# A hybrid retention and sliding-window layer on one core: the position bias table in and out of 128 partitions, and the projections' products and rotation sums moved from GpSimd to VectorE

## The chip, the core and the metric

The kernel runs on one core of a Trainium2 chip. The core has a TensorE (PE; its weight loads are listed apart, as PEld), a VectorE (DVE), a ScalarE (ACT), a GpSimd (POOL) and a SyncE (SP), which here issues most of the DMAs; 16 DMA engines move the data. The metric is the device time of one execution in microseconds; the time of a kernel is the median of its runs.

## What is computed

One step of a layer of width 1024 over 1024 prompt and 64 sample positions (1088 columns together), all in float32. What matters here is the first third of it: one combined projection of the normalized input, retention, and sliding-window attention with a relative position bias.

```python
def retention_qkv(rq, rk, rv, pos):
    q = rope(rq.reshape(B, S, RET_HEADS, RET_DK), pos)
    k = rope(rk.reshape(B, S, RET_HEADS, RET_DK), pos) * (RET_DK ** -0.5)
    v = rv.reshape(B, S, RET_HEADS, RET_DV)

def rope(x, pos):
    x1, x2 = xf[..., :half], xf[..., half:]
    return jnp.concatenate([x1 * cos - x2 * sin, x2 * cos + x1 * sin], axis=-1)

def in_proj(x, g_attn, w_in):
    return jnp.split(rms_norm(x, g_attn) @ w_in, SPLIT_OFFS, axis=-1)

def rel_bias_block(table, n_q, n_past):
    rel = (j - n_past) - i
    ...
    b = table[bucket]
    return jnp.transpose(b, (2, 0, 1)).reshape(SWA_KV_HEADS, SWA_GROUP, n_q, n_past + n_q)
```

Retention has 4 heads of 256; the window attention has 16 query heads of 64 on 2 key heads, a bias by distance from a table of 32 x 16 numbers, and a sink per head. Behind them follow gates, an output mix, cross attention to 256 memory rows, a SwiGLU of width 2816 and a last normalization.

## The kernel before

**The data.** Activations lie transposed: features on the 128 partitions, the 1088 columns along the free axis, in two halves of 544 columns. A float32 operand is split into a rounded part (ScalarE, L124) and the rest (VectorE, L125), and a product is three matmuls, one after the other (L223, L224, L226 for the large ones, L157 to L159 for the rest).

**The large projections** go in pairs of 128-row weight tiles through a Strassen scheme (`strassen`): seven products of 512 x 544 instead of eight. Sums of weight quarters (L191 to L197 on VectorE; L201 to L207 on GpSimd once `sums_by` is set to it) and their splits (wq) are made just ahead. A product fills a pair of PSUM banks called pq, of which there are three; it leaves them through a copy (ScalarE, L277) or a sum on VectorE (L274, L613), the latter into one of eight staging tiles called stage, each 128 x 544. A staging tile can be used anew when the store of what it held has landed.

**project_phase** makes, in the order of the code: v of head 0; then for each head h of 0 to 3 its k and q (`rotated`), for h > 0 its v, and one pair of the window attention's query rows (`project` with w_sq, stored to d_sq); the retention of that head (`retention`), block by block of 256 columns; at h = 1 the bias table, queued for a later moment; then the window attention's keys and values, the last query pair, and the gates. The retention of a head runs beside the projections of the next: its matmuls are mixed into PE's order among the large products, and its other steps into the orders of VectorE and ScalarE.

**Rotation** (`rotated`). With both rows a and b of a head's half in staging tiles, VectorE makes the four products with sine and cosine (L644 to L647). The difference (L649) and the sum (L650) are on VectorE for heads 0 and 1 and on GpSimd for heads 2 and 3. SP then stores both to d_qkv in DRAM, from where `retention` loads them as ks and qs, and the values as vf.

**The factor 1/rms** (rstd, spread over partitions by L512 and copied by ScalarE, L514) is multiplied to the window attention's queries, keys and values on GpSimd (L619, 20 instructions), and to the gates, which have an activation, on VectorE (the same line).

**Retention** of a block transposes ks and vf on PE (L768) into small PSUM banks (two of them, called r), from where ScalarE and VectorE scale and split them (L799, L800, L808, L809); then come the scores (pss), the state (pkv) and the output (po). `ret_out` normalizes the output through a chain of short VectorE steps (L893, L320 to L329) and ScalarE (L896), and PE transposes it back (L902).

**The bias table** (`bias_table`, L564 to L577): a one-hot matrix of 32 x 256 and the 32 x 16 table make 16 rows of 256 numbers, one per query head; they are scaled, written twice side by side (rb, 16 partitions of 2 KB) and stored 32 times over to d_rb, 16 rows of 64 KB. The window attention reads d_rb much later, with a row step that turns the repetition into the shift by distance.

**The order.** Tile, the layer that records the kernel, decides by its own model of times in which order instructions stand on each engine; each engine then goes through its order strictly, and so does SP with its DMAs. Hence moving an instruction from one engine to another can reorder the instructions around it on all engines.

Of the kernel before, what the change touches and what calls it, by code (L numbers as in the profile page):

```python
# [11 lines left out]
F32 = mybir.dt.float32  # L12
F32R = mybir.dt.float32r
AF = mybir.ActivationFunctionType
ALU = mybir.AluOpType
# [4 lines left out]
P = 128  # L20
# [7 lines left out]
BLK = 256  # L28
# [81 lines left out]
class Kernel:  # L110
# [453 lines left out]
    def bias_table(self):  # L564

        nc, io = self.nc, self.io
        t = self.ra.tile([P, BLK + 16], F32, tag="sf", bufs=1, name="table")
        rb = self.ra.tile([P, 2, BLK], F32, tag="o", bufs=1, name="rb")[:16]
        table, onehot = t[:32, BLK:], t[:32, :BLK]
        self.load(table, io["rel_bias"])  # L570
        self.load(onehot, io["c_onehot"])
        pb = self.norm_psum("pb")
        nc.tensor.matmul(pb[:16, :256], table, onehot, start=True, stop=True)
        nc.vector.tensor_scalar(rb, pb[:16, :256].unsqueeze(1).broadcast_to([16, 2, 256]), 8.0, None, ALU.mult)
        self.store(self.d_rb.rearrange("h (i c) -> h i c", c=512),
                   rb.rearrange("p a b -> p (a b)").unsqueeze(1).broadcast_to([16, 32, 512]))
        row = self.np.tile([P, 16], F32, tag="row", bufs=1, name="row")[:1]  # L577
        self.load(row, io["sinks"])
        ps = self.norm_psum("ps")
        nc.tensor.matmul(ps[:, :16], self.ones[:1, :], row, start=True, stop=True)  # L580
        for e in range(2):
            rows = slice(e * 64, (e + 1) * 64)
            nc.vector.tensor_copy(self.sinks[rows, :], ps[rows, :16].rearrange("p (a b) -> p a b", b=2)[:, :, e])
        self.minus = self.np.tile([P, 16], F32, tag="row", bufs=1, name="minus")[:, :NPAIR]
        nc.vector.tensor_scalar(self.minus, self.sinks, -1.0, None, ALU.mult)

    def project_phase(self):
        nc, tc, io = self.nc, self.tc, self.io
        with ExitStack() as ctx:
# [11 lines left out]
            half = lambda t: slice(t * HALF, (t + 1) * HALF)  # L601
# [14 lines left out]
            def project(w, put, act=None, other=None):  # L616
                def emit(i, t, ps, sb):
                    o = taken(ps, sb)
                    (nc.vector if act is not None else nc.gpsimd).tensor_tensor(  # L619
                        out=o, in0=o, in1=self.rstd[:, half(t)], op=ALU.mult)  # L620
                    if act is not None:
                        nc.scalar.activation(o, o, act)
                    if other is not None:
                        r = op.tile([P, HALF], F32, tag="other", bufs=4, name="other")
                        self.load(r, other(i)[:, half(t)])
                        nc.gpsimd.tensor_tensor(out=o, in0=o, in1=r, op=ALU.mult)
                    put(i, t, o)
                cast = self.last_cast
                self.strassen(w, self.ops, emit)
                return cast  # L630

            def rotated(w, h, j, before=None):
# [3 lines left out]
                def emit(i, t, ps, sb):  # L636
# [3 lines left out]
                    a, b = done[0, t], done[1, t]  # L640
                    cos, sin = (rope[:, i, half(t)] for i in range(2))
                    sa, sb = flat(staged()), flat(staged())
                    tt = nc.vector.tensor_tensor
# [1 line left out]
                    tt(out=sb, in0=b, in1=sin, op=ALU.mult)  # L645
                    tt(out=a, in0=a, in1=cos, op=ALU.mult)
                    tt(out=b, in0=b, in1=cos, op=ALU.mult)  # L647
                    tt = tt if h < 2 else nc.gpsimd.tensor_tensor
                    tt(out=a, in0=a, in1=sb, op=ALU.subtract)  # L649
                    tt(out=b, in0=b, in1=sa, op=ALU.add)  # L650
                    self.store(self.d_qkv[j, 2 * h, :, half(t)], a)
# [69 lines left out]
            for idx, w, act in ((1, "w_ga", AF.Sigmoid), (0, "w_rg", AF.Silu), (2, "w_gb", AF.Sigmoid)):  # L721
                for m in range(0, KT, 2):
                    if (idx, m) == (1, 6):
# [4 lines left out]
                        op = ctx.enter_context(tc.tile_pool(name="op", bufs=1, reuse_waits="tile"))  # L728
# [1164 lines left out]
```

## Time and profile before

| | us |
|---|---|
| median of 3 runs | 2172.07 (2171.89 to 2172.37) |
| the profiled execution | 2170.14 |
| its span | 2168.3 |
| PE busy | 2134.6 (98%) |
| DVE busy | 1547.7 (71%) |
| ACT busy | 875.0 (40%) |
| POOL busy | 588.8 (27%) |

The profile is of one execution; times in its views are microseconds from the start of its span. A row of a timeline has start, duration, engine, line, operation, tiles (out<-in) and, in brackets, how long the engine had been idle before and what ended that. A row of a group has the number of instructions, their busy time and mean duration in ns, and behind the second bar the idle time ahead of them with what ended it. Engines overlap instructions that follow each other, so that their starts can lie closer than a duration.

### The profile page before, as it was taken

Reading aid. Unit: us, or ns where it says so; the run is one execution under the profiler, and the core shown is the slowest. Engines: PE = TensorE matmul, PEld = TensorE weight load, DVE = VectorE, ACT = ScalarE, POOL = GpSimd, SP = SyncE. Lnnn points to the kernel's source line nnn. Section 1 sums busy time; section 2 is a strip of 40 time slices with the busy share of each in tenths; the row PEclk is TensorE's granted clock in tenths of the full one; section 3 lists DMA queues with packets and bytes.
Section 4 is the critical chain, followed back from the end, with each engine's and each line's share of the span. In section 5 each row is a group of like instructions: output and inputs, shape, how many; then the busy total and the mean of one; then the engine's idle time right before and its main releaser. Section 6 shows DMA issues by size and latency. Waiting matters only on the chain. (4 is left out here: it accounts for less than half of the span.)

```text
span 2168.3 us, 41740 instructions
## 1 busy us (share of the span) xinstructions
PE 2134.6 (98%) x16371; PEld 2082.8 (96%) x16371; DVE 1547.7 (71%) x2874; ACT 875.0 (40%) x1896; POOL 588.8 (27%) x484
## 2 busy tenths in 40 slices
PE   9999999999999999999999999999999999999997
PEld 9999999999999997889999999999999999999997
DVE  8986978776677558656545565778777777877597
ACT  8333434353434357543233333333322222344243
POOL 0001211233253124540000000015556555523531
PEclk9999999999999999999999999999999999999998
DMA  7334453444345476336442121522342333384333
GB/s 268 118 128 120 135 140 104 138 126 154 120 142 178 154 228 218 119 108 209 133 147 96 40 69 46 161 67 91 126 149 89 105 117 100 117 311 151 112 116 112
DMA packets 169894, 290.84 MB, mean 134 GB/s; under 512 B 39298, under 2 KB 96546, under 8 KB 169698
## 3 DMA queue, kind: packets, MB, share of 16 engines
q1 hardware_dynamic: 161666, 269.00, 38.8%
q0 software_dynamic: 3424, 10.82, 1.4%
q10 hardware_dynamic: 4608, 8.36, 1.0%
q8 instruction: 129, 2.11, 0.4%
q14 instruction: 67, 0.55, 0.1%
HBM read 196.95 MB, written 91.16 MB: 133 GB/s over the span
## 5 line engine op out<-in xcount | busy, mean ns | idle before, releaser
L125 DVE TENSOR_TENSOR wq<-raw,wq 128x512 fp32r<-128x512 f32 (+1 forms) x499 | 435.4, 877 | 131.8 <-ACT wq L124 128.2
L124 ACT CAST wq<-raw 128x512 fp32r<-128x512 f32 (+1 forms) x499 | 301.8, 614 | 539.8 <-PE pq L226 210.5
L224 PE MATMUL pq<-T,wq 128*128 128x272 f32 x1832 | 492.2, 289 | 0.1
L223 PE MATMUL pq<-T,wq 128*128 128x272 f32 x1832 | 490.7, 288 | 1.3 <-DVE stage L613 0.6
L224 PE MATMUL pq<-B,wq 128*128 128x272 f32 x1592 | 427.0, 288 | 0.1
L223 PE MATMUL pq<-B,wq 128*128 128x272 f32 x1592 | 425.7, 288 | 0.0
L226 PE MATMUL pq<-T,wq 128*128 128x272 f32 x1832 | 382.9, 289 | 1.9 <-DVE wq L125 1.9
L223 PEld LDWEIGHTS pq<-T,wq 128*128 128x128 f32 x1832 | 344.4, 188 | 2.1 <-ACT xsq L499 0.8
L224 PEld LDWEIGHTS pq<-T,wq 128*128 128x128 f32 x1832 | 344.2, 188 | 1.2 <-issue 0.8
L226 PE MATMUL pq<-B,wq 128*128 128x272 f32 x1592 | 331.7, 289 | 0.0
L224 PEld LDWEIGHTS pq<-B,wq 128*128 128x128 f32 x1592 | 299.1, 188 | 0.8 <-issue 0.4
L223 PEld LDWEIGHTS pq<-B,wq 128*128 128x128 f32 x1592 | 299.0, 188 | 0.1
L226 PEld LDWEIGHTS pq<-T,wq 128*128 128x128 f32 x1832 | 289.8, 189 | 3.9 <-DVE wq L125 2.4
L201 POOL TENSOR_TENSOR raw<-raw 128x512 f32<-128x512 f32 (+1 forms) x44 | 62.2, 1413 | 802.4 <-DVE rs_r L322 455.6
L226 PEld LDWEIGHTS pq<-B,wq 128*128 128x128 f32 x1592 | 251.7, 189 | 0.9 <-issue 0.7
L274 DVE TENSOR_TENSOR u<-pq,u 128x544 f32<-128x544 f32 x177 | 127.2, 719 | 84.8 <-PE pq L226 84.6
L619 POOL TENSOR_TENSOR stage<-stage,rstd 128x544 f32<-128x544 f32 x20 | 31.6, 1584 | 323.0 <-ACT rstd L514 203.7
L613 DVE TENSOR_TENSOR stage<-pq,u 128x544 f32<-128x544 f32 x112 | 80.3, 718 | 31.6 <-PE pq L226 27.8
L157 PE MATMUL pd<-xc,wq 128*128 128x256 f32 (+1 forms) x256 | 74.5, 291 | 0.0
L1541 POOL TENSOR_TENSOR stage<-stage,rstd_f 128x544 f32<-128x544 f32 x40 | 63.9, 1607 | 39.1 <-ACT stage L1540 39.1
L159 PE MATMUL pd<-xc,wq 128*128 128x256 f32 (+1 forms) x256 | 74.1, 290 | 0.0
L158 PE MATMUL pd<-xc,wq 128*128 128x256 f32 (+1 forms) x256 | 73.7, 288 | 0.0
(391 smaller groups left out, 4587.2 us busy)
## 6 DMA issues: line engine op xcount, KB each, us to landing
hl<-d_op SPq DMA_DIRECT2D x85, 272.0 KB, 5.1
d_qkv<-stage SPq DMA_DIRECT2D x44, 272.0 KB, 2.2
d_op<-stage SPq DMA_DIRECT2D x44, 272.0 KB, 2.5
d_op<-ht SPq DMA_DIRECT2D x44, 272.0 KB, 3.6
raw<-w_gate SPq DMA_DIRECT2D x22, 512.0 KB, 3.5
raw<-w_up SPq DMA_DIRECT2D x22, 512.0 KB, 5.1
raw<-w_down SPq DMA_DIRECT2D x16, 512.0 KB, 4.9
d_gate<-stage ACTq DMA_DIRECT2D x28, 272.0 KB, 2.8
```

The lines of the kernel that those rows point to most:

```text
L124: self.last_cast = self.nc.scalar.copy(hi, src).ins
L125: return self.nc.vector.tensor_tensor(out=lo, in0=src, in1=hi.bitcast(F32), op=ALU.subtract).ins
L157: mm(ps, wh, xh, start=start, stop=False)
L158: mm(ps, wh, xl, start=False, stop=False)
L159: self.last_mm = mm(ps, wl, xh, start=False, stop=stop).ins
L201: tt(out=a11, in0=a11, in1=a21, op=sub)
L223: mm(ps[:, c, :HC], w[:, 0, ks], x[:, 0, cs], start=start, stop=False)
L224: mm(ps[:, c, :HC], w[:, 0, ks], x[:, 1, cs], start=False, stop=False)
L226: self.last_mm = mm(ps[:, c, :HC], w[:, 1, ks], x[:, 0, c * HC:(c + 1) * HC], start=False, stop=stop).ins
L274: add = lambda out, a, b: nc.vector.tensor_tensor(out=out, in0=a, in1=b, op=ALU.add)
L613: nc.vector.tensor_tensor(out=o, in0=ps, in1=sb, op=ALU.add)
L1541: nc.gpsimd.tensor_tensor(out=g, in0=g, in1=r[t], op=ALU.mult)
```

## The change

It has three edits.

1. The table of the bias gets each of its columns 8 times in the input array (32 x 128 instead of 32 x 16), the matmul makes 128 rows instead of 16, and the scaled rows lie in 128 partitions. The store writes each partition 4 times over instead of 32, to the same 16 x 64 KB in the same order.
2. The products with rstd in `project` are on VectorE in all cases.
3. The rotation's difference and sum are on VectorE for all heads.

```diff
-        t = self.ra.tile([P, BLK + 16], F32, tag="sf", bufs=1, name="table")
-        rb = self.ra.tile([P, 2, BLK], F32, tag="o", bufs=1, name="rb")[:16]
+        t = self.ra.tile([P, BLK + P], F32, tag="sf", bufs=1, name="table")
+        rb = self.ra.tile([P, 2, BLK], F32, tag="o", bufs=1, name="rb")
         table, onehot = t[:32, BLK:], t[:32, :BLK]
...
-        nc.tensor.matmul(pb[:16, :256], table, onehot, start=True, stop=True)
-        nc.vector.tensor_scalar(rb, pb[:16, :256].unsqueeze(1).broadcast_to([16, 2, 256]), 8.0, None, ALU.mult)
-        self.store(self.d_rb.rearrange("h (i c) -> h i c", c=512),
-                   rb.rearrange("p a b -> p (a b)").unsqueeze(1).broadcast_to([16, 32, 512]))
+        nc.tensor.matmul(pb[:, :256], table, onehot, start=True, stop=True)
+        nc.vector.tensor_scalar(rb, pb[:, :256].unsqueeze(1).broadcast_to([P, 2, 256]), 8.0, None, ALU.mult)
+        self.store(self.d_rb.rearrange("h (r i c) -> (h r) i c", r=8, i=4),
+                   rb.rearrange("p a b -> p (a b)").unsqueeze(1).broadcast_to([P, 4, 512]))
...
-                    (nc.vector if act is not None else nc.gpsimd).tensor_tensor(
-                        out=o, in0=o, in1=self.rstd[:, half(t)], op=ALU.mult)
+                    nc.vector.tensor_tensor(out=o, in0=o, in1=self.rstd[:, half(t)], op=ALU.mult)
...
-                    tt = tt if h < 2 else nc.gpsimd.tensor_tensor
                     tt(out=a, in0=a, in1=sb, op=ALU.subtract)
                     tt(out=b, in0=b, in1=sa, op=ALU.add)
...
-    arr["rel_bias"] = a["rel_bias"]
+    arr["rel_bias"] = np.repeat(a["rel_bias"], 8, axis=1)
```

The lines behind the second edit stand one higher, those behind the third two higher: L644 to L647 become L643 to L646, the sums L649 and L650 become L647 and L648, and L768 becomes L766.

The orders of all engines differ between the place of the first moved product (at 204 us of the profile before) and the last one (at 499 us); ahead of it and behind it they are the same. Three places show how.

VectorE where the first query pair is projected (beside head 2's k). Before, its four products stand on GpSimd, and VectorE has:

```order
L125 TENSOR_TENSOR wq<-raw,wq 128x512
L193 TENSOR_TENSOR raw<-raw 128x512
L274 TENSOR_TENSOR u_3002<-pq,u_3000 128x544
L125 TENSOR_TENSOR wq<-raw,wq 128x512
L904 COPY ret_t<-pb 128x2x64
```

With the change:

```order
L125 TENSOR_TENSOR wq<-raw,wq 128x512
L193 TENSOR_TENSOR raw<-raw 128x512
L619 TENSOR_TENSOR stage_640<-stage_640,rstd 128x544 x4
L274 TENSOR_TENSOR u_3002<-pq,u_3000 128x544
L125 TENSOR_TENSOR wq<-raw,wq 128x512
L902 COPY ret_t<-pb 128x2x64
```

The four products now stand between a weight sum and the sum L274 that empties a bank.

VectorE a little later, at the rotation of head 2's first row pair, beside the retention of head 1. Before:

```order
L646 TENSOR_TENSOR stage_639<-stage_639,rope 128x544
L125 TENSOR_TENSOR wq<-raw,wq 128x512
L125 TENSOR_TENSOR qs<-qs 128x512
L125 TENSOR_TENSOR ss<-sf,ss 128x384
L645 TENSOR_TENSOR stage_640<-stage_640,rope 128x544
L125 TENSOR_TENSOR st<-state,st 128x512
L125 TENSOR_TENSOR wq<-raw,wq 128x512
L647 TENSOR_TENSOR stage_640<-stage_640,rope 128x544
L125 TENSOR_TENSOR ks<-ks 128x512
```

With the change (L645, L644 and L646 are the products above, L647 and L648 the sums):

```order
L645 TENSOR_TENSOR stage_639<-stage_639,rope 128x544
L648 TENSOR_TENSOR stage_639<-stage_639 128x544
L125 TENSOR_TENSOR qs<-qs 128x512
L644 TENSOR_TENSOR stage_640<-stage_640,rope 128x544
L125 TENSOR_TENSOR ss<-sf,ss 128x384
L647 TENSOR_TENSOR stage_639<-stage_639,stage_640 128x544
L125 TENSOR_TENSOR wq<-raw,wq 128x512
L646 TENSOR_TENSOR stage_640<-stage_640,rope 128x544
L647 TENSOR_TENSOR stage_639<-stage_639,stage_640 128x544
L125 TENSOR_TENSOR st<-state,st 128x512
L125 TENSOR_TENSOR ks<-ks 128x512
```

The sums stand among the splits of the retention of head 1 and of the weights. PE's order follows: the matmuls of head 1's retention stand further back among the large products (its last one behind 1920 matmuls of L223 to L226 instead of 1779), those of head 2 likewise, and from the retention of head 3 on they stand nearly where they stood.

SP around the store of the table (d_rb), with the query pair's stores (d_sq) and the loads of head 2's second block (vf, ks, qs). Before:

```order
L121 DMA d_ret<-ret_t 128x2x64
L121 DMA d_rb<-rb 512x1x512
L121 DMA d_sq<-stage_640 128x32
L121 DMA d_sq<-stage_640 128x8x64
L121 DMA d_sq<-stage_640 128x32
L121 DMA d_sq<-stage_640 128x8x64
L118 DMA vf<-d_qkv 128x2x256
L121 DMA d_sq<-stage_640 128x8x64
L121 DMA d_sq<-stage_640 128x32
L118 DMA raw<-w_q 128x1024
L118 DMA ks<-d_qkv 128x2x256
L118 DMA qs<-d_qkv 128x2x256
```

With the change:

```order
L121 DMA d_sq<-stage_640 128x8x64 x2
L121 DMA d_sq<-stage_640 128x32
L118 DMA raw<-w_q 128x1024
L121 DMA d_ret<-ret_t 128x2x256
L118 DMA table<-rel_bias 32x128
L118 DMA table<-c_onehot 32x256
L118 DMA raw<-w_q 128x1024
L121 DMA o_rss<-state 128x2x256
L121 DMA d_ret<-ret_t 128x2x64
L121 DMA d_rb<-rb 512x1x512
L118 DMA vf<-d_qkv 128x2x256
L118 DMA ks<-d_qkv 128x2x256
```

The query pair's stores and the loads of the next weight now stand ahead of the table's store, and the loads of head 2's second block directly behind it.

## The prediction

> **What bounds the kernel now.** I read the page first, then the busy times by stretch, then PE's waits in the stretch that the change touches. In the rows by stretch the columns are busy microseconds and instruction counts of PE, PEld, DVE, ACT and POOL, then granted clock, DMA share and GB/s.
>
> ```profile
> PE 2134.6 (98%) x16371; PEld 2082.8 (96%) x16371; DVE 1547.7 (71%) x2874; ACT 875.0 (40%) x1896; POOL 588.8 (27%) x484
> ```
>
> PE is busy for 98% of the span. The change removes no product from PE, so it can win only time in which PE stands still.
>
> ```profile
> 100.00:200.00 100.00, 100.00 (x800) 97.75 (x800) 80.04 (x167) 42.01 (x95) 0.00 (x0) 1.00 0.39 122
> 196.00:266.00 70.00, 67.41 (x536) 65.62 (x536) 61.77 (x109) 28.03 (x63) 19.18 (x12) 1.00 0.43 130
> 306.00:330.00 24.00, 21.59 (x174) 21.23 (x174) 14.98 (x26) 8.38 (x19) 5.22 (x3) 1.00 0.74 137
> 330.00:390.00 60.00, 59.89 (x490) 59.68 (x489) 54.62 (x106) 25.48 (x60) 12.96 (x8) 1.00 0.38 115
> 425.00:505.00 80.00, 80.00 (x653) 79.23 (x652) 59.46 (x112) 35.45 (x83) 28.34 (x19) 1.00 0.41 115
> 200.00:505.00 305.00, 299.05 (x2383) 291.29 (x2382) 237.64 (x454) 122.33 (x282) 69.05 (x44) 1.00 0.45 127
> ```
>
> All instructions that move off POOL stand between 200 and 505 us. There PE is idle for 305 - 299.05 = 5.95 us. This, 0.27% of the run, is about **all that can be won**. The clock is 1.00 in every row, so it is no term. PE's starts after a wait, in order of time:
>
> ```profile
> 231.21 0.63 PE L768 MATMUL pk<-ident,vf 128*128 128x128 f32 x4 [0.59 <-issue]
> 240.18 0.44 PE L902 MATMUL pb<-ident,ret_o 128*128 128x128 f32 x2 [0.32 <-ACT ret_o L896]
> 256.60 0.36 PE L157 MATMUL pss<-qs,ks 128*128 128x256 f32 x1 [0.58 <-DVE rr L322]
> 261.23 0.44 PE L902 MATMUL pb<-ident,ret_o 128*128 128x128 f32 x2 [1.11 <-ACT ret_o L896]
> 327.32 0.30 PE L768 MATMUL pk<-ident,ks 128*128 128x128 f32 x1 [2.41 <-DMA ks<-d_qkv]
> 405.06 0.44 PE L902 MATMUL pb<-ident,ret_o 128*128 128x128 f32 x2 [0.85 <-ACT ret_o L896]
> ```
>
> The brackets add up to 5.86 us. Four of the six (2.60 us) lie in 196 to 266, where GpSimd makes head 2's rotation sums; one (2.41) is a load; one (0.85) comes while GpSimd is idle.
>
> **The products and sums that move.** First what leaves GpSimd, and what the same sums cost on VectorE in the earlier heads:
>
> ```profile
> L619 POOL TENSOR_TENSOR stage<-stage,rstd 128x544 f32<-128x544 f32 x20 | 31.6, 1584 | 323.0 <-ACT rstd L514 203.7 <-DVE stage L613 90.9 <-issue 28.4
> L649 POOL TENSOR_TENSOR stage<-stage,stage 128x544 f32<-128x544 f32 x8 | 13.7, 1707 | 12.2 <-DVE stage L645 5.4 <-DVE rs_v L320 3.6 <-DVE stage L646 1.9
> L650 POOL TENSOR_TENSOR stage<-stage 128x544 f32<-128x544 f32 x8 | 12.8, 1596 | 83.7 <-DVE stage L644 57.7 <-DVE rs_t L324 22.6 <-DVE stage L647 2.7
> L649 DVE TENSOR_TENSOR stage<-stage,stage x8: 706/718/724, 62.5 to 135.6; 128x544 f32<-128x544 f32 x8
> 215.27 0.71 DVE L647 TENSOR_TENSOR stage<-stage,rope 128x544 f32<-128x544 f32 x1
> 215.91 0.70 DVE L613 TENSOR_TENSOR stage<-pq,u 128x544 f32<-128x544 f32 x1
> ```
>
> Here 20 products (L619) and 16 sums (L649, L650) leave GpSimd with 31.6 + 13.7 + 12.8 = 58.1 us. On VectorE such a sum takes 718 ns, but the last two rows, which follow without a gap, start 0.64 us apart, and that is what one adds to a full queue: 36 x 0.64 = **23.0 us of VectorE**, 12 of them (7.7 us) in 196 to 266 and 8 (5.1 us) in 330 to 390.
>
> What VectorE gets back is in its own long instructions. Groups of 100 to 200, when GpSimd did nothing, then of 196 to 266, then single instructions of both engines:
>
> ```profile
> L125 DVE TENSOR_TENSOR wq<-raw,wq 128x512 fp32r<-128x512 f32 x26 | 17.5, 685 | 3.7 <-ACT wq L124 3.7
> ...
> L125 DVE TENSOR_TENSOR wq<-raw,wq 128x512 fp32r<-128x512 f32 x15 | 13.3, 884 | 0.3 <-ACT wq L124 0.3
> L125 DVE TENSOR_TENSOR ks<-ks 128x512 fp32r<-128x512 f32 x3 | 4.2, 1393 | 0.0
> L646 DVE TENSOR_TENSOR stage<-stage,rope 128x544 f32<-128x544 f32 x4 | 3.6, 899 | 0.0
> L647 DVE TENSOR_TENSOR stage<-stage,rope 128x544 f32<-128x544 f32 x4 | 3.5, 882 | 0.0
> L125 DVE TENSOR_TENSOR st<-state,st 128x512 fp32r<-128x512 f32 x2 | 2.5, 1267 | 0.0
> L125 DVE TENSOR_TENSOR qs<-qs 128x512 fp32r<-128x512 f32 x2 | 2.5, 1266 | 0.0
> ...
> 248.83 1.90 POOL L650 TENSOR_TENSOR stage<-stage 128x544 f32<-128x544 f32 x1 [18.33 <-DVE stage L644]
> 250.69 1.82 POOL L649 TENSOR_TENSOR stage<-stage,stage 128x544 f32<-128x544 f32 x1
> ...
> 249.43 1.85 DVE L125 TENSOR_TENSOR ks<-ks 128x512 fp32r<-128x512 f32 x1
> 251.21 1.85 DVE L125 TENSOR_TENSOR st<-state,st 128x512 fp32r<-128x512 f32 x1
> 258.24 1.61 DVE L125 TENSOR_TENSOR wq<-raw,wq 128x512 fp32r<-128x512 f32 x1
> ```
>
> A VectorE instruction that reads two tiles of SBUF and begins under one of GpSimd's takes 1.85 instead of 0.685 us: GpSimd's first ends at 248.83 + 1.90 = 250.73, VectorE's 0.55 us later, at 249.43 + 1.85 = 251.28, as if it had stood until then; the next pair ends 0.55 us apart too. Against 685 ns (718 for the 544-wide) the six groups lose 15 x 0.199 + 3 x 0.708 + 4 x 0.181 + 4 x 0.164 + 2 x 0.582 + 2 x 0.581 = **8.8 us** in 196 to 266. The 12 added instructions cost 7.7 there. So VectorE's load stays about what it was (1.1 us less), and the sums end sooner: 0.64 us in VectorE's own order instead of about 1.7 us on GpSimd. The Trainium skill (SBUF — State Buffer, section "SBUF: two separate sides") says that VectorE and GpSimd share a port pair under an exclusive lock, held for the whole instruction. By its rule up to the whole 19.18 us of GpSimd in that stretch could come back; the sum goes by the 8.8 us of the rows.
>
> What this is worth on PE is read from the four waits. The chain before them is VectorE's (the kt, vb and root steps behind which a bank comes free and ret_o is scaled), and the instructions at 249.43, 251.21 and 258.24 stand ahead of the waits at 256.60 and 261.23 and are 1.17 + 1.17 + 0.93 us too long. For the steps without GpSimd I take 100 to 200: head 0's retention ran there beside head 1's rotations, all on VectorE, and PE was busy for 100.00 of 100 us. Bounds: none of the 2.60 us goes (other VectorE instructions now stand ahead), or all of it. **I take all, -2.6 us**, since the rows of 100 to 200 are the nearest case. The wait at 405.06 is not GpSimd's:
>
> ```profile
> 416.71 1.68 POOL L619 TENSOR_TENSOR stage<-stage,rstd 128x544 f32<-128x544 f32 x1 [28.40 <-issue]
> ```
>
> GpSimd is idle for 28.4 us before 416.7, so I leave these 0.85 us as they are. Bounds: gone, or, as another place of the new order may be as tight, one more wait like the longest of this kind (1.11).
>
> The four products of the first query pair (L619 x4) now stand in VectorE's order behind L193. They wait for rstd, and behind them wait a bank sum (L274) and the split of a weight:
>
> ```profile
> 204.12 5.80 POOL L619 TENSOR_TENSOR stage<-stage,rstd 128x544 f32<-128x544 f32 x4 [203.67 <-ACT rstd L514]
> 206.41 0.72 DVE L274 TENSOR_TENSOR u<-pq,u 128x544 f32<-128x544 f32 x1 [2.09 <-PE pq L226]
> ```
>
> rstd is there at 204.12, and until 206.41 VectorE sits idle, waiting for PE. Four products take 4 x 0.64 = 2.6 us and end 0.3 us late; this I cost at nothing, since the slowing by GpSimd's four, which run for 5.80 us, goes. Without the idle time it would be 2.6 us.
>
> On SP the stores of products and sums come sooner; loads behind them wait less.
>
> **The bias table.** The matmul, the scaling and the two loads cost what they did (same columns, 128 partitions instead of 16 of the same engines). The store is another matter. Its issue, the stretch while it runs, and one in which other transfers filled the DMA engines:
>
> ```profile
> 306.54 0.67 SPq L121 DMA_DIRECT2D d_rb<-rb  x1
> d_rb<-rb SPq DMA_DIRECT2D x1, 1024.0 KB, 12.7
> ...
> 308.00:318.00 10.00, 10.00 (x81) 9.83 (x81) 8.06 (x15) 3.53 (x8) 5.08 (x3) 1.00 0.91 100
> 324.00:326.00 2.00, 0.91 (x8) 0.70 (x6) 0.13 (x1) 0.00 (x0) 0.00 (x0) 1.00 0.94 335
> ...
> 322.10 0.54 SPq L118 DMA_DIRECT2D ks<-d_qkv  x1
> ```
>
> 1 MB out of 16 partitions holds the engines at a share of 0.91 for 10 us and moves 100 GB/s; tiles of 128 partitions go at 335 GB/s at the same share. At that rate the store takes 1049 KB / 335 GB/s = 3.1 us (an estimate). Bounds: 10 us as now, or 3.1. I take 3.1, since every other store of 128 partitions moves so. Behind the old store stood query stores, a weight and, issued at 322.10, ks of head 2's second block, for which PE waits 2.41 us until 327.32. With the engines free 7 us earlier, and the query stores now ahead of the table's, ks comes in time: **-2.4 us**; bounds 0 and -2.41. The Trainium skill (SBUF — State Buffer, section "Door 1: The DMA port swizzle") counts a transfer's speed by the SBUF ports that its partitions reach; 16 partitions reach a quarter, so the store would take 2.5 us, an estimate from that page. Against it stands the last rival.
>
> **The sum.** -2.6 - 2.4 = -5.0 us. The profiled execution took 2170.14 us (span 2168.3 and 1.84 around it), so it would take 2165.1. The median of the runs, 2172.07, is 1.93 above it: **2167.1 us**, 0.23% faster. From 505 us on the order of the instructions is the same, and I take nothing there.
>
> **The rivals.**
> - *Only the load is mended.* VectorE has as much to do as before, so PE waits at other places for as long: -2.4, 2169.7 us. For it: VectorE is busy for 61.77 of 70 us. Against it: in the row below VectorE is fuller and PE never waits.
>
> ```profile
> 100.00:125.00 25.00, 25.00 (x205) 25.00 (x205) 24.51 (x48) 11.04 (x25) 0.00 (x0) 1.00 0.34 119
> ```
>
> - *VectorE becomes the bound (slower).* If the long instructions are long for another reason than GpSimd, nothing comes back: VectorE would need 61.77 + 7.7 = 69.5 of 70 us and 54.62 + 5.1 = 59.7 of 60. From the point at which added work exceeds the idle time (8.2 and 5.4 us), bank sums come late, all banks of the products are full, and PE goes at VectorE's pace: +12.8 for the 20 instructions, -2.4 for the load, 2182.5 us. The ends of the pairs above speak against it.
> - *Nothing moves.* The load comes late for SP's order, not for the store, and the waits return elsewhere: 2172.1 us.
> - *The store stays slow.* Its source rows are each read several times; if that limits it, ks is as late as now: -2.6, 2169.5 us. The Trainium skill (DMA: Bandwidth & Descriptors, "Why a DMA increments its semaphore by 16 and not by 1") sets the number of DMA engines by the outermost sizes, and by that both stores get all 16. The share of 0.91 agrees for the old store.
>
> **How the numbers follow.** Chances: forecast 0.56, only the load 0.18, store slow 0.08, nothing 0.06, VectorE the bound 0.12. A measurement of this kernel tells about 0.2% (4.3 us, so below 2167.7 or above 2176.4) from no change. The forecast counts as faster (0.56), the three next as the same (0.32), the last as slower (0.12). The range: at best all 5.86 us of brackets go, and 0.15 us more at each of six, since a bracket begins at a modelled end: 2165.3, and I go 1 us lower for small waits, 2164.3. At the top it takes in "nothing" and one new wait of 1.11: 2173.2. That leaves out the slower case.
>
> **What would show it.** Right: VectorE's splits and rotation products at 0.69 and 0.72 us all through 200 to 390; the table's store landing in some 5 us; no PE wait for ks; idle of PE between 200 and 505 about 1 us. Wrong: PE waits for wq or pq released by VectorE in 200 to 270 (VectorE the bound); splits of 1.8 us with GpSimd idle; a store at 100 GB/s; or new waits for ret_o of 1 us and more where the retention steps now stand.

## The result and the profile after

| | before | after |
|---|---|---|
| median of 9 runs each, us | 2171.89 (2168.96 to 2172.37) | 2165.95 (2161.74 to 2167.79) |
| the profiled execution | 2170.14 | 2166.56 |
| its span | 2168.3 | 2164.8 |

The ratio is 0.997, 95% interval 0.9962 to 0.9979: faster by 0.3%, 5.9 us between the medians, where 5.0 were forecast. The busy line and the rows by stretch of the changed kernel, with the columns as in the prediction:

```profile
PE 2136.7 (99%) x16371; PEld 2085.8 (96%) x16371; DVE 1555.2 (72%) x2910; ACT 875.0 (40%) x1896; POOL 530.9 (25%) x448
```

```profile
196.00:266.00 70.00, 70.00 (x563) 69.02 (x562) 62.16 (x125) 28.00 (x62) 0.00 (x0) 1.00 0.43 128
306.00:330.00 24.00, 24.00 (x170) 21.11 (x170) 17.92 (x38) 7.43 (x16) 0.00 (x0) 1.00 0.47 148
330.00:390.00 60.00, 60.00 (x493) 60.00 (x492) 53.56 (x107) 26.51 (x62) 0.00 (x0) 1.00 0.40 127
200.00:505.00 305.00, 305.00 (x2428) 297.10 (x2427) 244.81 (x503) 127.72 (x291) 11.66 (x8) 1.00 0.44 132
```

The last row is the answer to the 5.95 us of idle time: PE is now busy for all of the 305 us. VectorE has 36 more instructions in the whole run (2910 instead of 2874) but is hardly busier (1555.2 instead of 1547.7), and in 196 to 266 only by 0.4 us. Its groups in that stretch show why:

```profile
L125 DVE TENSOR_TENSOR wq<-raw,wq 128x512 fp32r<-128x512 f32 x17 | 11.6, 683 | 0.3 <-ACT wq L124 0.3
...
L125 DVE TENSOR_TENSOR ks<-ks 128x512 fp32r<-128x512 f32 x3 | 2.0, 682 | 0.0
```

The splits are back at 683 and 682 ns (884 and 1393 before). The table's store, first its issue and landing, then the DMA engines while it runs (the last two columns are their busy share and GB/s):

```profile
d_rb<-rb SPq DMA_DIRECT2D x1, 1024.0 KB, 4.5
```

```profile
322.00:323.00 1.00, 1.00 (x10) 1.00 (x9) 1.00 (x2) 0.59 (x1) 0.00 (x0) 1.00 1.01 389
323.00:324.00 1.00, 1.00 (x11) 1.00 (x10) 0.97 (x2) 0.00 (x0) 0.00 (x0) 1.00 1.02 377
```

1 MB now moves at 377 to 389 GB/s and lands after 4.5 us instead of 12.7. Everything expected of the stretch came. But the profiled execution is only 3.58 us shorter. I compared the start of the same numbered product of PE in both traces: the 4400th, at 564.01 us before, starts 7.13 us sooner, the one at 664.02 6.23 sooner, at 982.39 5.74, at 1178.47 3.16, the last 3.56. The largest piece lost lies between 982 and 1178, where PE waits for nothing; one group of each, before and after, from 1000 to 1180 us:

```profile
L157 PE MATMUL pd<-mix,wq 128*128 128x384 f32 x128 | 43.1, 336 | 0.0
```

```profile
L157 PE MATMUL pd<-mix,wq 128*128 128x384 f32 x128 | 43.4, 339 | 0.0
```

The same matmuls took 339 instead of 336 ns, at a granted clock of 1.00 in both. Whether that belongs to the changed kernel was the first thing to try.

### The profile page after: what moved, and what is told of

It is laid out like the page before. It is cut to its first block, busy times and chain, and to the rows that moved or that the text cites. A ratio compares the mean times of both kernels' runs of the same rounds, so it can differ in the third digit from the quotient of the medians.

```text
span 2164.8 us, 41721 instructions
## 1 busy us (share of the span) xinstructions
PE 2136.7 (99%) x16371; PEld 2085.8 (96%) x16371; DVE 1555.2 (72%) x2910; ACT 875.0 (40%) x1896; POOL 530.9 (25%) x448
## 4 chain that ended last, share of the span: by engine, by line
PE 88%; DVE 6%; DMA 2%; issue 2%; ACT 1%; POOL 1%; SPq 0%; POOLq 0%; DVEq 0%; ACTq 0%
PE pq L226 18%; PE pq L223 17%; PE pq L224 17%; PE pd L157 8%; PE pd L159 8%; PE pd L158 8%; DVE wq L125 1%; PE pout L1067 1%; PE pss L1004 1%; PE pk L766 1%; DMA hl<-d_op 1%; PE pp L1043 1%; DVE T L125 1%; DMA swin<-d_gate 1%; PE po L159 1%
## 5 line engine op out<-in xcount | busy, mean ns | idle before, releaser
L125 DVE TENSOR_TENSOR wq<-raw,wq 128x512 fp32r<-128x512 f32 (+1 forms) x499 | 429.4, 865 | 138.4 <-ACT wq L124 134.9
L223 PE MATMUL pq<-T,wq 128*128 128x272 f32 x1832 | 490.6, 287 | 1.5 <-ACT wq L124 0.6
L223 PE MATMUL pq<-B,wq 128*128 128x272 f32 x1592 | 425.4, 287 | 0.2 <-ACT stage L621 0.2
L226 PE MATMUL pq<-T,wq 128*128 128x272 f32 x1832 | 382.7, 289 | 1.9 <-DVE wq L125 1.9
L201 POOL TENSOR_TENSOR raw<-raw 128x512 f32<-128x512 f32 (+1 forms) x44 | 63.6, 1446 | 1259.3 <-DVE wq L125 496.2
L223 PEld LDWEIGHTS pq<-T,wq 128*128 128x128 f32 x1832 | 344.3, 188 | 3.3 <-issue 1.8
L226 PE MATMUL pq<-B,wq 128*128 128x272 f32 x1592 | 331.9, 289 | 0.0
L223 PEld LDWEIGHTS pq<-B,wq 128*128 128x128 f32 x1592 | 298.9, 188 | 0.5 <-ACT stage L621 0.4
L226 PEld LDWEIGHTS pq<-T,wq 128*128 128x128 f32 x1832 | 289.6, 189 | 3.6 <-DVE wq L125 2.4
L226 PEld LDWEIGHTS pq<-B,wq 128*128 128x128 f32 x1592 | 251.7, 189 | 0.9 <-issue 0.7
L274 DVE TENSOR_TENSOR u<-pq,u 128x544 f32<-128x544 f32 x177 | 127.2, 719 | 75.4 <-PE pq L226 75.0
L204 POOL TENSOR_TENSOR raw<-raw 128x512 f32<-128x512 f32 (+1 forms) x44 | 58.9, 1338 | 53.1 <-DVE wq L125 50.6
```

The costliest lines, as they stand in the source:

```text
L125: return self.nc.vector.tensor_tensor(out=lo, in0=src, in1=hi.bitcast(F32), op=ALU.subtract).ins
L201: tt(out=a11, in0=a11, in1=a21, op=sub)
L223: mm(ps[:, c, :HC], w[:, 0, ks], x[:, 0, cs], start=start, stop=False)
L226: self.last_mm = mm(ps[:, c, :HC], w[:, 1, ks], x[:, 0, c * HC:(c + 1) * HC], start=False, stop=stop).ins
L274: add = lambda out, a, b: nc.vector.tensor_tensor(out=out, in0=a, in1=b, op=ALU.add)
```

## The experiments

**My theory**: GpSimd's two-input instructions keep VectorE's waiting, VectorE's steps then come late for PE (four waits), and the store from 16 partitions makes ks late (one wait). **Rivals**: the waits went because the order of the instructions is another one; or only one of the two edits does it all.

**The changed kernel again.** No edit.

> The changed kernel as it is, for a second profile. The profile on hand shows PE 7.1 us ahead of the kernel before at 564 us, but only 3.2 us ahead from 1180 us on, without a wait in between: matmuls of 128x384 take 339 instead of 336 ns there. Theory: this loss belongs to the execution, not to the kernel. Then this profile has 336 ns again and a span of about 2161 to 2162 us, and the median is 2164 to 2167. Rival: the kernel does it (another place of something in memory or time); then 339 ns again and a span of 2164 to 2166.

Median 2164.11 us, ratio 0.9964 (0.9951 to 0.9976), span 2165.4. Its group from 1000 to 1180 us:

```profile
L157 PE MATMUL pd<-mix,wq 128*128 128x384 f32 x128 | 43.0, 336 | 0.0
```

336 ns again, and between 874 and 1900 us the lead shrinks by only 0.23 us: the slow matmuls belonged to that one execution. The span that I expected was too short, though. PE was 6.80 us ahead at 564 us, but 5.64 at 664 and 3.18 at 817. The second loss has a wait at its place, in this run and in the kernel before:

```profile
801.07 0.69 PE L157 MATMUL pd<-ret,wq 128*128 128x384 f32 x1 [3.17 <-ACT swin L1200]
```

```profile
805.92 0.45 PE L157 MATMUL pd<-ret,wq 128*128 128x384 f32 x1 [0.89 <-ACT swin L1202]
```

Here the window attention begins, and PE waits for a step on its inputs, 3.17 us instead of 0.89. From 800.46 to 807.29 the granted clock is 0.50; the kernel before has half as much of that, a little earlier (its rows stand further below). In the first profile of the changed kernel the wait at this place is 0.61. So of what is won before 505 us a part can be given back later, another part in each execution.

**Only the table in 128 partitions.** The products and sums stay on GpSimd, and the order of every engine is that of the kernel before.

```
 def bias_table: as in the changed kernel
 project, rotated: as before
```

> The table alone in 128 partitions; products and sums stay on GpSimd, and the order of all engines is that of the kernel before. Theory (the slow store holds the DMA engines and so delays ks): the store lands in 4 to 5 us, PE's wait of 2.41 us for ks goes, the other five waits (3.45 us) stay; idle of PE between 200 and 505 us 3.5 us, time 2.4 us below the kernel before. Rival (ks is late by SP's order, behind the query stores that wait for GpSimd): the store is short too, but the wait for ks stays above 1.5 us and the time is within 1 us of before.

Median 2169.16 us, ratio 0.9986 (0.9977 to 0.9995): a gain of 2.4 us. The waits of PE that are left between 195 and 510:

```profile
231.69 0.63 PE L768 MATMUL pk<-ident,vf 128*128 128x128 f32 x4 [0.65 <-issue]
256.86 0.36 PE L157 MATMUL pss<-qs,ks 128*128 128x256 f32 x1 [0.58 <-DVE rr L322]
261.49 0.44 PE L902 MATMUL pb<-ident,ret_o 128*128 128x128 f32 x2 [1.11 <-ACT ret_o L896]
402.33 0.44 PE L902 MATMUL pb<-ident,ret_o 128*128 128x128 f32 x2 [0.67 <-ACT ret_o L896]
```

The wait for ks is gone; of the other five the small one at 240 (0.32) went and four stand. This edit alone did what its term said.

**Only products and sums on VectorE**, with the old table. The order is that of the changed kernel.

```
 def bias_table: as before
 project, rotated: as in the changed kernel
```

> Products and sums on VectorE; the table as before, 16 partitions. The order of all engines is that of the changed kernel. Theory: VectorE's splits take 0.69 us, none of the ret_o, pss and vf waits is left, the store holds the DMA engines for 10 us again, and PE waits 1 to 3 us for the loads behind it (vf, ks of head 2's second block); time 3.5 to 5 us below the kernel before. Rival (the order alone mends it, since the query stores now stand ahead of the table's): no wait of PE between 200 and 505 us at all, and the time is that of the changed kernel, about 6 us below.

Median 2164.66 us, ratio 0.9966 (0.9954 to 0.9978). The store was slow again (it landed after 12.3 us), but it cost nothing. The row of the stretch, and SP's issues of the table and of the loads behind it:

```profile
200.00:505.00 305.00, 304.59 (x2425) 296.60 (x2424) 243.37 (x500) 127.69 (x291) 11.70 (x8) 1.00 0.46 132
```

```profile
320.76 0.66 SPq L121 DMA_DIRECT2D d_rb<-rb  x1
325.23 0.36 SPq L118 DMA_DIRECT2D vf<-d_qkv  x1
332.26 0.36 SPq L118 DMA_DIRECT2D ks<-d_qkv  x1
```

My theory failed, and its rival, that the order alone mends the load, held: in the new order no weight is issued right behind the store, and ks follows only 11.5 us later. Each edit alone wins 2.4 and 6.9 us against the 5.9 and 7.5 of both together, so the gains don't add up.

**Only the sums, and only the products on VectorE**, both with the old table.

```diff
 sums alone (the products' line as before):
-                    tt = tt if h < 2 else nc.gpsimd.tensor_tensor
 products alone (the sums' line as before):
-                    (nc.vector if act is not None else nc.gpsimd).tensor_tensor(
+                    nc.vector.tensor_tensor(
```

> The old table and its store out of 16 partitions; the 16 rotation sums of heads 2 and 3 on VectorE; the 20 products with 1/rms of the SWA projections stay on GpSimd. Theory (what costs PE time is GpSimd reading two tiles of SBUF just ahead of PE's tight places, and between 225 and 262 us that is the sums alone): the four waits of 196 to 266 go as they did with both moved; GpSimd keeps about 32 us of busy time; PE between 200 and 505 us is busy for 303.5 to 304.6 us; splits of VectorE stay long only where a product runs (about 204 to 210, 330 to 390, 416 to 500). Median 2165.5 to 2168 (the kernel with both moved and the old table: 2164.7; before: 2171.6). Rival (every GpSimd instruction costs PE a like share): about half of the gain of both, 302 us of PE and 2168 to 2169.5.

> The old table and its store; the 20 products with 1/rms on VectorE; the 16 rotation sums of heads 2 and 3 stay on GpSimd. Theory (the sums between 225 and 262 us are what PE waits for): waits for ret_o and rr of 0.3 to 1.1 us stay between 225 and 262, the ks wait of about 2.4 us stays unless SP's order moved, and a split of ks or st that begins under a sum still takes 1.85 us. PE between 200 and 505 us is busy for 299.5 to 301.5 us, median 2169 to 2171.6. Rival (the products in SP's and VectorE's order are what mends it): no wait in 196 to 266, PE over 303 us, median below 2168.

Neither is faster: 2169.72 us, ratio 0.9994 (0.9983 to 1.0005), and 2171.87 us, 1.0004 (0.9994 to 1.0015). In 196 to 266 PE was busy for 70.00 and for 69.89 us, so both lost the four waits there. With the sums alone a new wait appeared at the store. From its trace: SP's issue of the table and of the weight behind it, the cast of that weight on ScalarE, VectorE's split, PE's wait, and, in a fence of their own, the stretches from there, where the third number from the right is the granted clock:

```profile
312.99 0.67 SPq L121 DMA_DIRECT2D d_rb<-rb  x1
314.10 0.35 SPq L118 DMA_DIRECT2D raw<-w_q  x1
...
327.86 1.14 ACT L124 CAST wq<-raw 128x512 fp32r<-128x512 f32 x2 [7.45 <-DMA raw<-w_q]
...
328.52 0.69 DVE L125 TENSOR_TENSOR wq<-raw,wq 128x512 fp32r<-128x512 f32 x1 [6.56 <-ACT wq L124]
...
332.34 0.58 PE L157 MATMUL po<-vb,ss 128*128 128x256 f32 x1 [3.89 <-ACT ss L124]
```

```profile
332.00:336.00 4.00, 3.66 (x17) 3.67 (x18) 4.00 (x8) 2.84 (x6) 0.00 (x0) 0.50 0.00 0
336.00:340.00 4.00, 4.00 (x28) 4.00 (x28) 4.00 (x9) 1.71 (x7) 0.00 (x0) 0.81 0.02 4
```

The weight stands right behind the store and lands 13.7 us after its issue; VectorE, which goes through its order strictly, sits idle for 6.56 us before the weight's split, and the step that scales the scores (sf, at 331.00), whose cast ss PE waits for, stands behind that. When PE resumes, its clock is 0.50, then 0.81: a loss of 3.66 x 0.50 + 4.00 x 0.19 = 2.6 us on top of the 3.89. With the products alone the wait is 3.30 us, and the clock behind it 0.57:

```profile
328.00:332.00 4.00, 3.46 (x17) 3.46 (x18) 2.58 (x7) 0.27 (x2) 0.00 (x0) 0.57 0.34 120
```

That is 3.46 x 0.43 = 1.5 us more. The 2.41 us of the kernel before had no such sequel (1.00 in all its rows from 320 to 345). The Trainium skill (TensorE: Matmul & The Clock Gate, "What's actually happening") says that the clock falls to half after an idle window of about 3.4 us, counted on a window that runs free, and comes back after as long a busy one. In these traces a window that is idle only in part is enough: with the sums alone the clock fell at 330.68, 2.2 us into the wait, and in every run it falls at the beginning of the window attention, in the kernel before after waits of 0.82 and 1.01 us. The 3.4 us ahead of the fall and the stretch behind it, with the sums alone, then in the kernel before:

```profile
327.27:330.68 3.41, 1.17 (x10) 0.95 (x8) 1.67 (x3) 1.14 (x2) 0.00 (x0) 1.00 0.63 232
330.68:337.50 6.82, 5.16 (x23) 5.17 (x24) 6.82 (x13) 4.36 (x12) 0.00 (x0) 0.50 0.00 0
```

```profile
794.12:797.53 3.41, 1.59 (x20) 1.23 (x18) 2.52 (x11) 3.32 (x7) 0.00 (x0) 1.00 0.89 272
797.53:800.94 3.41, 3.41 (x19) 3.33 (x16) 0.00 (x0) 3.39 (x8) 1.08 (x2) 0.50 0.37 127
```

So the length of a single wait does not tell whether the clock falls; the clock in the rows behind it does.

Both halves of the edit, then, win the waits in 196 to 266, and both, by the order that follows from them, put a weight behind the slow store. To test that, each was given the new table. The order of every engine is that of the run without it.

> The run with the rotation sums alone on VectorE, given the new table in 128 partitions as well; apart from the size of the table's instructions every engine has the same order as in that run, so the store alone differs. Theory (there the slow store cost 3.9 us of waiting, since a weight for the products was issued right behind it, and some 2.5 us more because matmuls behind the wait started 0.21 instead of 0.12 us apart for 5 us): the weight behind the store lands 4 to 6 us sooner, no PE wait over 0.5 us between 200 and 505, granted clock 1.00 in every row, PE busy for 304 to 305 of 305 us; median 2164 to 2167 (sums alone: 2169.7). Rival (the sums alone are worth little, and the wait for ss comes from the new order of VectorE): a wait of 2 us or more stays there, 2168 to 2169.5.

> The run with the 20 products alone on VectorE, given the new table in 128 partitions as well; the order of every engine is that of the run without it. Theory (the store's stall hid what the products bring): the wait of 3.3 us for vb and the slow matmuls behind it go, PE is busy for 303.5 to 305 of 305 us with the clock at 1.00; median 2164.5 to 2167.5 (products alone: 2171.9). The sums left on GpSimd still stretch splits of ks, st and qs to 1.2 to 1.85 us, and a wait or two of 0.2 to 1 us may stay. Rival (the sums on GpSimd cost PE 2 to 3 us wherever they stand): PE below 303 us, median over 2168.

Sums and table: 2162.93 us, ratio 0.9966 (0.9952 to 0.998). Products and table: 2166.07 us, 0.9976 (0.9962 to 0.999). The stretch in the one and in the other:

```profile
200.00:505.00 305.00, 305.00 (x2425) 296.73 (x2424) 237.47 (x479) 128.20 (x291) 42.51 (x28) 1.00 0.44 131
```

```profile
200.00:505.00 305.00, 305.00 (x2428) 297.39 (x2428) 243.84 (x484) 127.92 (x292) 38.20 (x24) 1.00 0.44 133
```

No idle time of PE in either, and in the first, where the weight is issued 1.1 us behind the store as it was with the old table, its cast comes at 320.15 instead of 327.86. SP's two issues and ScalarE's cast:

```profile
312.86 0.60 SPq L121 DMA_DIRECT2D d_rb<-rb  x1
313.96 0.35 SPq L118 DMA_DIRECT2D raw<-w_q  x1
...
320.15 0.61 ACT L124 CAST wq<-raw 128x512 fp32r<-128x512 f32 x1
```

The stall of the store is shown: same order, another store, 6.8 us of time (2169.72 to 2162.93, on two chips on which the kernel before took 2170.84 and 2170.91). But the second run speaks against my theory of the four waits. The sums are still on GpSimd, and VectorE's splits still wait for them; of its GpSimd and VectorE:

```profile
249.69 1.82 POOL L648 TENSOR_TENSOR stage<-stage,stage 128x544 f32<-128x544 f32 x1
...
250.20 1.85 DVE L125 TENSOR_TENSOR st<-state,st 128x512 fp32r<-128x512 f32 x1
```

and yet PE doesn't wait. The long instructions that are left just ahead of the waits are not enough, in this order, to make them. What differs earlier is the four products at 204 us, beside which two splits of VectorE took 1.84 and 1.64 us with the table alone. Hence the next run.

**The table and the first four products only.**

```diff
-                        project(pair("w_sq", h - 1), queries(h - 1))
+                        project(pair("w_sq", h - 1), queries(h - 1), first=h == 1)
 (first: on VectorE; all other products and all sums as before)
```

> The new table, and of the 36 instructions only the first four products with 1/rms (those of the first query pair, at about 204 us) on VectorE; the other 16 products and all 16 sums stay on GpSimd. Theory (the four waits of 196 to 266 are a debt made at 204 to 210: with these four on GpSimd two of VectorE's splits there take 1.84 and 1.64 us, 2.1 us too much, and VectorE comes to the tight place at 256 us about 1.3 to 1.5 us later than in the run with all products moved): splits between 204 and 211 take 0.68 us, the root that PE waits for at 256 is done 1 us or more sooner, PE is busy for 69.8 us or more of the 70 from 196 to 266 although splits under the sums still take 1.2 to 1.85 us; over 303.5 of 305 us in all, median 2165 to 2168. Rival (the sums at 219 to 260 make the waits, and the runs with the products moved lost them by their new order alone): waits of 0.6 to 1.1 us for ret_o and rr stay, PE about 302 us, median about 2169 (table alone: 2169.2).

Median 2169.22 us, ratio 0.9989 (0.998 to 0.9999). Its stretches and its waits of PE between 195 and 510:

```profile
196.00:266.00 70.00, 69.89 (x562) 68.60 (x561) 63.73 (x117) 28.63 (x64) 13.27 (x8) 1.00 0.46 136
...
330.00:390.00 60.00, 57.01 (x465) 56.63 (x464) 52.99 (x102) 24.93 (x57) 12.63 (x8) 1.00 0.39 121
```

```profile
378.66 0.36 PE L157 MATMUL pss<-qs,ks 128*128 128x256 f32 x1 [1.12 <-DVE rr L322]
389.38 0.35 PE L157 MATMUL po<-vb,ss 128*128 128x256 f32 x1 [1.86 <-DVE ret_t L904]
```

In 196 to 266 what the theory of a debt expected came: with four instructions moved the waits there are gone (69.89 of 70), and the last step of the root that PE waited for begins at 258.45 instead of 260.67 us, although the split of st still takes 1.85. But that does not show the theory, since the order is planned anew here too. VectorE's rows with the table alone, then in this run:

```profile
258.49 1.61 DVE L125 TENSOR_TENSOR wq<-raw,wq 128x512 fp32r<-128x512 f32 x1
...
260.67 0.16 DVE L329 TENSOR_TENSOR rr<-rr,tok 128x2 f32<-128x2 f32 x1
```

```profile
258.45 0.16 DVE L329 TENSOR_TENSOR rr<-rr,tok 128x2 f32<-128x2 f32 x1
258.53 0.68 DVE L125 TENSOR_TENSOR wq<-raw,wq 128x512 fp32r<-128x512 f32 x1
```

A weight's split stood ahead of the root's last three steps and held them up by 1.53 us (the next step begins at 260.02); now a split stands behind them. So a good part of the 2.22 us can be the order. Nor is the debt enough by itself to make the waits: in the run with the sums and the table the first four products are still on GpSimd, and a split beside them is still long,

```profile
204.11 5.76 POOL L619 TENSOR_TENSOR stage<-stage,rstd 128x544 f32<-128x544 f32 x4 [203.65 <-ACT rstd L514]
...
207.04 1.60 DVE L125 TENSOR_TENSOR wq<-raw,wq 128x512 fp32r<-128x512 f32 x1
```

and the four waits are gone there all the same. Either half taken off GpSimd clears the stretch, each in an order of its own; no run sets the order apart from the time that GpSimd costs VectorE.

In the total the theory failed, and the rival's 2169.2 us came, though by waits that it did not name: two of 1.12 and 1.86 us stand now in head 3, where the kernel before had none. GpSimd works for 12.63 us there, against 13.09 with all products moved and 12.96 before, both without a wait. So it is not how long GpSimd works that decides in head 3. That leaves where the new order puts the steps; which step it is, no run tells apart.

**GpSimd's reading by itself.** Behind the rotations of heads 2 and 3 in the changed kernel, GpSimd does work for which nobody waits: in the one run 16 sums of two tiles, in the other 16 copies of one tile (its expectation says 32; there are two for each of eight rotations). The order is planned anew, and much alike: on VectorE some 50 of its 2910 places differ between the changed kernel and the run with sums, and some 100 between the two runs.

```diff
                     tt(out=b, in0=b, in1=sa, op=ALU.add)
+                    sums:   sa = sa + sb; sb = sb + sa, on GpSimd, for h > 1
+                    copies: sa = sb; sb = sa, on GpSimd, for h > 1
```

> The changed kernel, and after each rotation of heads 2 and 3 GpSimd adds the two finished sine products to each other twice, 128x544 each (16 instructions, results unused, nobody waits for them but the next user of those staging tiles). Theory (GpSimd's reading slows VectorE): VectorE's two-tile instructions that begin under these take 1.2 to 1.9 us again, VectorE loses 8 to 14 us between 200 and 400 us, and waits of PE come back, 1 to 3 us between 200 and 400; time 1 to 3 us above the changed kernel. Rival (the slow sums stood in the way themselves, and the longer instructions were harmless, or the new order gives PE slack): VectorE's instructions are long but PE waits less than 0.5 us.

> The changed kernel with 32 copies on GpSimd (one tile of SBUF read, one written, 128x544, nobody waits for them) behind the rotations of heads 2 and 3, in place of the 16 two-input sums of the earlier run. Theory A (it is any access of GpSimd to SBUF that keeps a two-input instruction of VectorE waiting): VectorE's splits that begin under a copy take 1 us or more, VectorE's busy time between 200 and 505 us is 5 us or more above the changed kernel's 244, and PE loses 2 us or more. Theory B (only instructions of GpSimd with two tiles as input do that): splits stay at 0.68, VectorE's busy time within 1 us of 244, and PE busy for 304 us or more.

The sums: 2168.08 us, ratio 0.9983 (0.9974 to 0.9993). The copies: 2167.61 us, one run. First the stretch with the sums, then the longest of its six waits, then the stretch with the copies, and last the copies (min, median and max of one, in ns):

```profile
200.00:505.00 305.00, 301.30 (x2398) 293.62 (x2397) 255.15 (x493) 123.54 (x285) 42.19 (x24) 1.00 0.43 129
```

```profile
381.23 0.44 PE L900 MATMUL pb<-ident,ret_o 128*128 128x128 f32 x2 [0.96 <-DVE stage L613]
```

```profile
200.00:505.00 305.00, 305.00 (x2430) 297.52 (x2429) 245.99 (x503) 128.53 (x291) 34.91 (x25) 1.00 0.44 132
```

```profile
L648 POOL COPY stage<-stage x16: 640/1033/5776, 221.9 to 374.8; 128x544 f32<-128x544 f32 x16
```

With the sums VectorE is busy for 255.15 instead of 244.81 us, with no instruction of its own more, and PE loses 3.70 us: in nearly the same order, GpSimd's sums beside VectorE bring such waits back. With the copies PE loses nothing, as theory B had it, and VectorE's 245.99 us are 1.2 above the changed kernel's 244.81, a little more than B allowed. B's reason isn't shown, though: a copy takes 0.64 us alone, so it can't hold VectorE for long, and here it was mostly the copies that were held up (5.78 us the longest). That the run with the copies is not faster than 2167.61 us comes later: PE's lead of 7.17 us at 564 falls to 4.27 at 817, where the wait at the window attention takes 3.99 us.

**The store from 64 and from 32 partitions**, in the changed kernel.

```diff
-        nc.tensor.matmul(pb[:, :256], table, onehot, start=True, stop=True)
+        nc.tensor.matmul(pb[:64, :256], table, onehot, start=True, stop=True)
-        self.store(self.d_rb.rearrange("h (r i c) -> (h r) i c", r=8, i=4),
+        self.store(self.d_rb.rearrange("h (r i c) -> (h r) i c", r=4, i=8),
 (cut: the scaling, the tiles and the input array follow; with 32, r=2, i=16)
```

> The changed kernel with the bias table held in 64 partitions instead of 128: 8 source rows read per partition, the same 1 MB and the same packets of 2 KB. Theory A (the store is bound by how many ports of SBUF its partitions reach, and 64 neighbouring partitions reach half of them): about 5 us of moving and a landing of 6.5 to 7.5 us, and with 32 partitions about the same. Theory B (each partition is read at its own rate, 16 partitions at 100 GB/s): 64 partitions at up to 400 GB/s, so no slower than 128, landing 4.5 us, and 32 partitions about 200 GB/s, landing 6.5 to 7.5. The ks wait does not come back under either; PE between 200 and 505 us within 0.5 us of 304.9.

> The changed kernel with the bias table in 32 partitions: 16 reads of each row, the same bytes and packets. Theory A (ports): 32 neighbouring partitions reach as many ports as 64, so the landing is that of 64 partitions within 0.7 us. Theory B (rate per partition): half as fast as 64 partitions, landing 6.5 to 7.5 us where 64 lands in 4.5. Were neither right and a rate fixed by the number of descriptors in flight, all of 16, 32 and 64 would land in about 12.5. PE between 200 and 505 us within 0.5 us of 304.9 in each case.

One run each, 2164.76 and 2165.46 us. The landing and two microseconds of the store from 64 partitions, then the same two from 32:

```profile
d_rb<-rb SPq DMA_DIRECT2D x1, 1024.0 KB, 7.1
```

```profile
324.00:326.00 2.00, 2.00 (x19) 2.00 (x18) 1.80 (x4) 1.38 (x3) 0.00 (x0) 1.00 0.93 197
```

```profile
d_rb<-rb SPq DMA_DIRECT2D x1, 1024.0 KB, 7.2
```

```profile
324.50:326.50 2.00, 2.00 (x18) 2.00 (x17) 1.75 (x4) 1.56 (x4) 0.00 (x0) 1.00 0.93 197
```

PE is busy for 304.83 and 304.15 of the 305 us; the wait of 0.8 us in the second, which I had not expected, is for a step of VectorE (ret_t), not for a load. 64 partitions are no faster than 32: 197 GB/s in both, against 100 from 16 and 377 to 389 from 128. A rate per partition (theory B) would have made 64 twice as fast as 32. The Trainium skill (SBUF — State Buffer, "Door 1: The DMA port swizzle") says that neighbouring partitions reach ports in such a way that 64 get no more of them than 32, half of the sixteen; the three steps of 100, 197 and 377 to 389 agree with a quarter, a half and all of them.

**All together** (PE's idle time between 200 and 505 us; each ratio is to runs of the kernel before on the same chip):

| table from | on VectorE | idle of PE, us | median, us | ratio (95%) |
|---|---|---|---|---|
| 16 | nothing | 5.95 | 2171.89 | |
| 128 | nothing | 3.11 | 2169.16 | 0.9986 (0.9977 to 0.9995) |
| 128 | first 4 products | 3.10 | 2169.22 | 0.9989 (0.998 to 0.9999) |
| 16 | products | 3.60, and 1.5 by the clock | 2171.87 | 1.0004 (0.9994 to 1.0015) |
| 128 | products | 0.00 | 2166.07 | 0.9976 (0.9962 to 0.999) |
| 16 | sums | 3.89, and 2.6 by the clock | 2169.72 | 0.9994 (0.9983 to 1.0005) |
| 128 | sums | 0.00 | 2162.93 | 0.9966 (0.9952 to 0.998) |
| 16 | both | 0.41 | 2164.66 | 0.9966 (0.9954 to 0.9978) |
| 128 | both (the change) | 0.00 | 2165.95 | 0.997 (0.9962 to 0.9979) |

No run is better than the change by more than the intervals allow. The sums with the table have the lowest median, and the 20 products are not shown to bring anything beside them.

## Why the prediction was right, and where it was not

**What bounds the kernel** was right: the idle time of 5.95 us between 200 and 505 was what could be won, and all of it went. At 564 us PE is even 7.13 and 6.80 us ahead; the prediction's upper bound (5.86 us of brackets and 0.15 more at each of six) is 6.8.

**The four waits, -2.6.** The size was right, all four went. The step behind it is not shown: I put the waits down to the three long instructions at 249.43, 251.21 and 258.24. With the sums alone moved these are short and the waits gone, as I had it. But with the first four products moved, st still takes 1.85 and ks 1.28 us at this place, and the waits are gone too. So the four products that I cost at nothing, at 204 to 210, matter as much, by their own time on GpSimd or by the order that follows from them. Which of the two it is stays open.

**The load, -2.4.** Right for the kernel's old order: the table alone won 2.4 us of the median and the wait for ks. But it is no property of the store. Its price is what stands behind it: ks in the old order (2.41), a weight with the sums (3.89 and 2.6 by the clock), nothing in the order of the change (0.41 us of idle time in all, none of it at the store). My sum of two terms came out right because each was near what it measured in the old order; as a sum it is wrong, since the edit on VectorE alone brings nearly all. That the total came so near is in part luck: 7.13 and 6.80 us were won in the two profiles, and what was lost again behind 564 us, which I had at nothing, took 3.6 and 3.9 of it.

**The wait at 405** I left as it was (0.85). It went with the rest, so idle of PE was 0 where I expected 1 us.

**The store's 3.1 us** of moving was nearly right: 1049 KB at 377 to 389 GB/s are 2.7 to 2.8 us, and it landed in 4.5 us where I wrote some 5. My estimate of 2.5 from the Trainium skill (SBUF — State Buffer, "Door 1: The DMA port swizzle") was as near. I misread the row for the rate, though: every store whose landing is on record had landed by 323.91, and what was in flight from 324 to 326 were loads (a weight, ks and qs). So 335 GB/s was no rate of a store. The rival that the repeated reading of source rows holds it is out: twice the reads of each row, 16 instead of 8, leave the rate at 197 GB/s.

**VectorE's load** was right in kind: 36 more instructions and, from 200 to 505, 244.81 instead of 237.64 us, so most of their 23.0 us came back. VectorE as the bound did not come: busy for 62.16 of 70 us and 53.56 of 60.

**Nothing from 505 us on**: this was wrong in both executions. 3.6 and 3.9 us of the lead at 564 us were lost again by the end, in the one mostly by slow matmuls, in the other mostly at the beginning of the window attention. The medians, 5.9 us apart, say that on the whole less is lost.

## What to carry to other kernels

A slow transfer costs what stands behind it on its queue, and an edit that reorders the queue can set that to nothing or double it: test such an edit with and without the other before adding up terms. Do not take the last long instructions before a wait for its cause without a test: they can stay and the wait go, when an edit some 50 us ahead plans the order anew; compare which steps stand ahead of the awaited one in both orders. And a wait of PE can cost more than its length: behind 3.30 and 3.89 us the matmuls at half clock lost 1.5 and 2.6 us more.

## What the runs showed that I had not expected

After pauses of 3.30 and 3.89 us PE resumed at half clock, for about 3 and 5 us; after 2.41 it did not. At the beginning of the window attention the clock fell in every run, in the kernel before behind waits of 0.82 and 1.01 us. A store from 64 partitions is as slow as from 32 (7.1 and 7.2 us to landing). And for one execution the same matmuls took 339 instead of 336 ns for about 200 us at a granted clock of 1.00; no run tells why.
